# Earlier tile chains in the output projection, and seven products in place of eight for the second gate and up block

## The chip, the cores and the metric

The kernel runs on one core of a Trainium2 chip. The metric is the device time of one execution in microseconds (us). A core has several engines that run side by side, each working through its own list of instructions in order: TensorE (PE in the profile) multiplies matrices, VectorE (DVE) and ScalarE (ACT) work on elements, GpSimd (POOL) does a few small things here, and SyncE's queue (SP) starts the transfers from memory.

## The reference

One layer of a hybrid network, on 128 prompt tokens and 512 sample tokens, in float32, width 1024. Cut to what matters here:

```python
h = _rms(x, norm_mix) * (1 + sc1) + sh1
mix, k, v = _mixer(h, ...)               # attention and a short convolution, then merged @ w_out
x = x + g1 * mix
h2 = _rms(x, norm_ffn) * (1 + sc2) + sh2
gate, up = jnp.split(h2 @ w_gate_up, 2, axis=-1)      # w_gate_up: 1024 x 5632
x = x + g2 * ((jax.nn.silu(gate) * up) @ w_down)      # w_down: 2816 x 1024
```

## The kernel before

All 640 tokens are handled together, as five tiles of 128 in the order prompt, 0, 1, 2, 3 (`TORD`; below they are the first to the fifth tile). Every float32 matrix is split into a high and a low part (`split`: ScalarE rounds the high part, VectorE subtracts to get the low part), and every product is three matmuls (`mm3`: high by high, high by low, low by high).

**The output projection** runs in two halves of 512 columns (`for j in range(2)`). In the second half (j = 1), for each tile n, TensorE does 24 matmuls into `ab`; then comes what is called a tile chain here: ScalarE scales one half (L1070), VectorE adds the other (L1071), multiplies by the gate `g1` (L1073) and adds the residual (L1074); ScalarE sums the squares (L1079), VectorE, GpSimd and VectorE make the norm (L159, L161, L1081) and leave `x2n`. After the matmuls of tile n, TensorE transposes `x2n` of tile n - 1 (`h2_turn`, L960), and ScalarE (L967) or VectorE (L965, four of the last tile's eight pieces) evicts the pieces with the modulation into `h2`. So the fourth tile's transposes come after the fifth tile's matmuls, and the last tile's transposes come inside the gate and up stage.

**Gate and up** treats 22 blocks f of 128 gate and 128 up columns. Per block, the weights are a 2 by 2 matrix of blocks (A11, A12 for gate, A21, A22 for up; the inner dimension halved) and the activations another (B11 and B21 for tokens 0 to 319, B12 and B22 for tokens 320 to 639). A product of one A block and one B block is 12 matmuls of 320 columns. The first `NPLAIN` = 2 blocks go by the eight plain products (`plain`, once for the low tokens `LO`, once for the high ones `HI`). The others go by seven products (Strassen and Winograd's form): `ff_a` A11 by B11, `ff_c` S1 by T1, `ff_d` S2 by T2, `ff_b` A12 by B21, `ff_e` S3 by T3, A22 by T4 and S4 by B22, `ff_end` the last sums. S1 to S4 are sums of weight blocks, made by VectorE for each f (L203) and split (L147, L148); T1 to T4 are sums of activation blocks, made once (`b_sums`: L1033, then split by L1019 and L1020). `b_plain` splits the B blocks themselves (L1017, L1019, L1020). B12, B22 and T1 to T4 are made in two parts: `two[0]`, tokens 320 to 511, once the fourth tile is there, and `two[1]`, tokens 512 to 639, once the fifth is there.

TensorE's order is written out by hand. At the start of gate and up it is, as the program says it:

```python
b_plain("B12 B22", two[0]); b_sums(two[0])
for x in range(NPLAIN):
    plain(x, ("B11", "B21"), LO)
    if x == 0:
        h2_turn(TORD[-1])
        b_plain("B12 B22", two[1])
b_sums(two[1])
for x in range(NPLAIN):
    plain(x, ("B12", "B22"), HI)
```

(two lines joined in one; the third block, f = 2, follows by seven products.) The orders of VectorE and ScalarE are not written by hand: when the program is built, each engine takes, among the instructions whose inputs are expected to be there, the one that stands first in the program. `early(n)` counts an instruction as if it stood n places earlier. A chain of dependent instructions on one engine lets a waiting one of lower rank in between its links. What is built is a fixed list for each engine.

Weights come through SP's queue into three buffers of 512 KB (`wf`) and are split into eight slots (`wh`, `wl`) in a planned order (`order`, `W`, `op_load`); the same eight slots hold the output projection's weights until its last matmuls. The splits of the first block and of A11 of the second are placed in the program ahead of the chains of the later tiles.

Of the kernel before, what the change touches and what calls it, by code (L numbers as in the profile page):

```python
# [28 lines left out]
HALF = TOK // 2  # L29
# [23 lines left out]
GSP = 30  # L53
FEND = 2
AOP = 9
NPLAIN = 2
QEV = '00001'
PPO = ''
RSP = 0
# [9 lines left out]
PT = 2  # L69
PRB = 4  # L70
PHB = 2
XP = 50
AWB = 2
AO = 6
SOON = 150
# [12 lines left out]
def build(ctx, tc, x_prompt, x_sample, c, cache_k, cache_v, c_ctx, norm_mix, norm_ffn, w_ada, b_ada,  # L88
# [27 lines left out]
    def T(tag, shape, dt=F32, bufs=1):  # L116
        seq[0] += 1
        return pools[where.get(tag, "A")][1].tile(list(shape), dt, tag=tag, bufs=bufs, name=f"{tag}_{seq[0]}")
# [15 lines left out]
    def PS2():  # L134
        return PB((P, 2, 512), tag="s")
# [7 lines left out]
    def early(n):  # L143
        return tc.high_priority(n)

    def split(hi, lo, src):
        act.activation(hi, src, AF.Copy)  # L147
        dve.tensor_tensor(lo, src, f32(hi), ALU.subtract)  # L148

    def mm3(out, lh, ll, rh, rl, start, stop, more=False):  # L150
        pe.matmul(out, lh, rh, start=start, stop=False, skip_group_check=more)  # L151
        pe.matmul(out, lh, rl, start=False, stop=False, skip_group_check=more)  # L152
        pe.matmul(out, ll, rh, start=False, stop=stop, skip_group_check=more)  # L153
# [31 lines left out]
    def plan(key, src, ph=0, ring="w", gain=None):  # L185
        place[key] = len(order)
        order.append([key, src, ph, ring, gain, None])
# [3 lines left out]
    def op_load(e):  # L191
# [4 lines left out]
        if name[0] == "S":  # L196
            if name == "S1":
# [3 lines left out]
                             "S3": (s13, a11, a21, ALU.subtract), "S4": (s24, a12, s24, ALU.subtract)}[name]  # L201
            with early(SOP[f >= NPLAIN]):
                (pool if f < SPO else dve).tensor_tensor(src, x, y, op)  # L203
# [3 lines left out]
        ops[0] += 1  # L207
        with early(SOP[f >= NPLAIN]):
            split(w[:, 0], w[:, 1], src)
# [72 lines left out]

    GROUPS = [list(range(a, b)) for a, b in zip(GCUT, GCUT[1:])]
    PLAIN, PRODS = ("A11", "A12", "A21", "A22"), ("A11", "S1", "S2", "A12", "S3", "A22", "S4")

    def plan_raw(f, x, ph=3):
        col = f * P + (DFF if x == "u" else 0)
        plan((x, f), wg[:, :, col:col + P], ph, "f")

    def plan_ops(f, names, ph=3):  # L290
        for x in names:
            plan(("op", f, x), None, ph, "op")

    G2KP = {0: (0,), 1: (1,), 2: (2, 3)}
    for gi, grp in enumerate(GROUPS):
        for f in grp:
            ph = 2 if f < NPLAIN else 3
            plan_raw(f, "g", ph)
            plan_raw(f, "u", ph)
            plan_ops(f, PLAIN if f < NPLAIN else PRODS, ph)  # L300
        for j in range(2):
            for i0 in range(0, len(grp), 2):
                n = len(grp[i0:i0 + 2])
                plan(("d", grp[i0], j), wd[:, grp[i0]:grp[i0] + n, j * 512:(j + 1) * 512], 2)
                if gi == 0 and j == 0:
                    for kp in G2KP[i0 // 2]:
                        plan(("ada", 5, 1, kp), wa[:, 2 * kp:2 * kp + 2, 5 * D + 512:6 * D], 2, "f")
# [614 lines left out]
    for x in SEQ.split():  # L922
        if "." in x:
            n, i = (int(y) for y in x[1:].split("."))
# [44 lines left out]
    def mix_half(src):  # L969
        mh = T("mH", (P, 4, P), F32R, 4)  # L970
        ml = T("mL", (P, 4, P), F32R, 4)
        split(mh, ml, src)
        return mh, ml
# [34 lines left out]
    def quarter(name, part):  # L1008
        h, c0 = int(name[1]) - 1, HALF * (int(name[2]) - 1)
        return h2[h][:, :, c0 + part.start:c0 + part.stop]  # L1010

    def b_put(name, src, part):
        if name not in B:
            b_tile(name)
        w = B[name][4]
        if name in BHD:
            dve.tensor_copy(w[:, 0, :, part], src)  # L1017
        else:
            act.activation(w[:, 0, :, part], src, AF.Copy)  # L1019
        dve.tensor_tensor(w[:, 1, :, part], src, f32(w[:, 0, :, part]), ALU.subtract)  # L1020

    def b_plain(names, part):
        for x in names.split():
            b_put(x, quarter(x, part), part)

    def b_sums(part):
        n = part.stop - part.start
        b11, b12, b21, b22 = (quarter(x, part) for x in ("B11", "B12", "B21", "B22"))
        last = None
        for x in ("T1", "T2", "T3", "T4"):  # L1030
            w = T("tr", (P, 4, 192), F32, 3)[:, :, :n]
            y, z = {"T1": (b12, b11), "T2": (b22, last), "T3": (b22, b12), "T4": (b21, last)}[x]
            dve.tensor_tensor(w, y, z, ALU.subtract)  # L1033
            b_put(x, w, part)
            if x != "T3":
                last = w

    for j in range(2):
        cols = slice(j * 512, (j + 1) * 512)
        for n, t in enumerate(TORD):  # L1040
            cc = 1 if t == CTX else 0
            c0 = t * P + (2 if t == CTX else 0)
            ms = [mix_ctx if t == CTX else mix_half(of[t]), mix_half(yf[:, :, c0:c0 + P])]
            ab = PS2()
            for half in range(2):
                for p in range(4):
                    wh, wl = W(("o", j, 2 * half + p // 2))
                    mm3(ab[:, half], ms[half][0][:, p], ms[half][1][:, p], wh[:, p % 2], wl[:, p % 2],
                        p == 0, p == 3)
                if j == 0 and CRP == f"{n}{'me'[half]}":  # L1050
                    next(ada_gen, None)
                    conv_rms()
            if j == 1 and n:
                h2_turn(TORD[n - 1])
                if n == 2:
                    b_plain("B11 B21", slice(0, 256))
                if n == 3:
                    b_plain("B11 B21", slice(256, HALF))
            if j == 0 and n == 1:
                att_rms(NL - 1)  # L1060
            if j == 0 and G2N <= n < 4 + G2N:
                g2_step(0, n - G2N)
            if j == 1 and n == 0:
                g2_out(0)
            if j == 0:
                x2[t] = T("x2", (P, D), F32, NT)
                sp.dma_start(x2[t], x_dram[t])
            with early(XP):
                m = T("mix", (P, 512), F32, 2)
                act.activation(m, ab[:, 1], AF.Copy, scale=rB[t])  # L1070
                dve.scalar_tensor_tensor(m, ab[:, 0], rA[t], m, ALU.mult, ALU.add)  # L1071
                e = pool if j == 0 and n < PX else dve
                e.tensor_tensor(m, m, g1[cc][:, cols], ALU.mult)  # L1073
                e.tensor_tensor(x2[t][:, cols], m, x2[t][:, cols], ALU.add)  # L1074
            if j == 1:
                with early(XP):
                    x2n[t] = T("x2n", (P, D), F32, 1)
                    ss = T("ss", (P, 1), F32, 6)
                    act.activation(x2n[t], x2[t], AF.Square, accum_out=ss)  # L1079
                    r = rstd_of(ss, 1, 1.0 / D)  # L1080
                    dve.tensor_scalar_mul(x2n[t], x2[t], r)  # L1081
# [49 lines left out]
    def ff_a(f):  # L1131
        b1 = FB()
        prod(b1, f, "A11", "B11")
        cg = T("cg", (P, TOK), F32, 2)
        st[f] = [b1, copy_of("p1", b1), cg, None, None, None, None]

    def ff_b(f):
        b2 = FB()
        prod(b2, f, "A12", "B21")
        b1, p1, cg = st[f][0:3]  # L1140
        dve.tensor_tensor(cg[:, LO], b2[:, :HALF], p1, ALU.add)
        act.activation(cg[:, LO], cg[:, LO], AF.Silu)
# [69 lines left out]
    for gi, grp in enumerate(GROUPS):  # L1212
        for f in grp:
            if f == 0:
                two = slice(0, 192), slice(192, HALF)
                b_plain("B12 B22", two[0])
                b_sums(two[0])
# [3 lines that stand above are left out]
                        h2_turn(TORD[-1])  # L1221
                        b_plain("B12 B22", two[1])
                        phase[0] = 3
                b_sums(two[1])
                for x in range(NPLAIN):
                    plain(x, ("B12", "B22"), HI)
            elif f >= NPLAIN:
                ff_a(f)
                if f - 1 in st and FEND == 1:
                    ff_end(f - 1)  # L1230
                ff_c(f)
                if f - 1 in st:
                    ff_end(f - 1)
                ff_d(f)
                ff_b(f)
                ff_e(f)
                if f == grp[-1] or FEND == 0:
                    ff_end(f)
        down(gi, grp)
        for f in grp:  # L1240
            del gT[f]
# [52 lines left out]
```

## Time and profile before

| | us |
|---|---|
| median of 3 runs | 765.26 (763.04 to 766.77) |
| the profiled execution's own time | 765.82 |
| its span | 764.1 |
| TensorE busy | 739.6 |
| VectorE busy | 560.2 |
| ScalarE busy | 374.4 |

Times in the trace are counted from the span's start. 1.72 us of the execution lie outside the span. A line of the timeline gives the start, the duration, the engine, the line of the kernel, the operation, its result and its operands, and in brackets how long the engine had been idle and what ended that. Matmuls overlap, so the distance between two starts is what one costs, not the printed duration; the same holds, for under 0.1 us, on VectorE and ScalarE. The change concerns the stretch from about 314 us (the fourth tile's chain) to 357.5 us (start of the block f = 2).

### The profile page before, as it was taken

To read this page: it belongs to the slowest core of one execution; us is meant where nothing else is said; L and a number is where in the kernel's file an instruction comes from. 1 tells how busy PE (TensorE), PEld (TensorE's weight loads), DVE (VectorE), ACT (ScalarE), POOL (GpSimd) and SP (SyncE) were. 2 spreads that over 40 slices of the span, in tenths; PEclk is the share of its full clock that TensorE was granted. 3 is DMA by queue.
4 is the path that set the end of the run, shared out by engine and by line. 5 is a ranking of instruction groups with operands and counts; after the bars stand their busy time and mean duration, and the time that the engine had idled before them with its cause. 6 is when DMAs were issued, how large, how long until landed. Compare 5 with 4: busy or idle time off the path is not lost.

```text
span 764.1 us, 11890 instructions
## 1 busy us (share of the span) xinstructions
PE 739.6 (97%) x4580; PEld 665.5 (87%) x4580; DVE 560.2 (73%) x1009; ACT 374.4 (49%) x712; POOL 48.2 (6%) x77
## 2 busy tenths in 40 slices
PE   4998999999999999899999999999999999999997
PEld 3667988989999887699998789998889998899986
DVE  5566987676566798798779678884578866788653
ACT  5355776666665445865552125553125541255410
POOL 3104201011010130000000000000000000000000
PEclk9999999999999999989999999999999999999999
DMA  9984133423424453121235313233113232222312
GB/s 289 301 241 140 42 111 112 152 90 113 151 90 133 157 179 112 53 59 56 84 109 164 99 56 111 65 102 111 55 56 98 69 111 75 64 84 83 111 55 83
DMA packets 102349, 84.52 MB, mean 111 GB/s; under 512 B 4526, under 2 KB 82674, under 8 KB 102292
## 3 DMA queue, kind: packets, MB, share of 16 engines
q1 hardware_dynamic: 100980, 83.39, 35.8%
q8 instruction: 36, 0.59, 0.3%
q10 hardware_dynamic: 1056, 0.26, 0.2%
q14 instruction: 21, 0.17, 0.1%
q0 software_dynamic: 256, 0.11, 0.1%
HBM read 79.68 MB, written 2.75 MB: 108 GB/s over the span
## 4 chain that ended last, share of the span: by engine, by line
PE 85%; DVE 6%; DMA 3%; ACT 2%; SPq 1%; POOL 1%; issue 1%; ACTq 0%; DVEq 0%; POOLq 0%
PE pf L151 19%; PE pf L153 19%; PE pf L152 19%; PE pc L674 3%; PE pc L675 3%; PE pc L676 3%; PE po L831 2%; PE ps L788 2%; PE pt L814 2%; PE pc L376 2%; DMA af<-in_w_ada_dram 2%; PE ps L151 2%; PE ps L152 2%; PE ps L153 2%; POOL rs L161 1%
## 5 line engine op out<-in xcount | busy, mean ns | idle before, releaser
L147 ACT ACTIVATE wh<-wf 128x1024 fp32r<-128x1024 f32 (+1 forms) x76 | 64.1, 844 | 93.6 <-PE pf L153 63.0
L151 PE MATMUL pf<-wh,gT 128*128 128x512 f32 (+1 forms) x225 | 88.2, 392 | 0.0
L152 PE MATMUL pf<-wl,gT 128*128 128x512 f32 (+1 forms) x225 | 87.8, 390 | 0.0
L153 PE MATMUL pf<-wh,gT 128*128 128x512 f32 (+1 forms) x225 | 87.8, 390 | 0.0
L148 DVE TENSOR_TENSOR wl<-wf,wh 128x1024 fp32r<-128x1024 f32 (+1 forms) x42 | 49.2, 1171 | 29.7 <-ACT wh L147 26.8
L674 PE MATMUL pc<-hH,wh 128*128 128x320 f32 x192 | 61.1, 318 | 0.0
L676 PE MATMUL pc<-hH,wl 128*128 128x320 f32 x192 | 59.4, 309 | 0.0
L675 PE MATMUL pc<-hL,wh 128*128 128x320 f32 x192 | 59.4, 309 | 0.0
L152 PEld LDWEIGHTS pf<-wl,gT 128*128 128x128 f32 x225 | 42.3, 188 | 9.8 <-DVE wl L148 0.2
L151 PEld LDWEIGHTS pf<-wh,gT 128*128 128x128 f32 x225 | 42.2, 188 | 9.9 <-ACT wh L147 0.2
L153 PEld LDWEIGHTS pf<-wh,gT 128*128 128x128 f32 x225 | 42.2, 188 | 9.8
L151 PE MATMUL pf<-T,wl 128*128 128x320 f32 x160 | 49.2, 308 | 0.0
L152 PE MATMUL pf<-T,wl 128*128 128x320 f32 x160 | 49.2, 308 | 0.0
L153 PE MATMUL pf<-T,wl 128*128 128x320 f32 x160 | 49.2, 308 | 0.0
L151 PE MATMUL pf<-T,wh 128*128 128x320 f32 x160 | 49.2, 308 | 0.0
L152 PE MATMUL pf<-T,wh 128*128 128x320 f32 x160 | 49.2, 308 | 0.0
L153 PE MATMUL pf<-T,wh 128*128 128x320 f32 x160 | 49.2, 307 | 0.0
L151 PE MATMUL pf<-B,wl 128*128 128x320 f32 x152 | 47.0, 309 | 0.0
L152 PE MATMUL pf<-B,wl 128*128 128x320 f32 x152 | 46.8, 308 | 0.0
L153 PE MATMUL pf<-B,wl 128*128 128x320 f32 x152 | 46.7, 307 | 0.0
L1207 DVE TENSOR_TENSOR dm<-pf,g 128x512 f32<-128x512 f32 (+1 forms) x41 | 27.7, 675 | 22.9 <-PE pf L153 22.9
L147 ACT ACTIVATE wl<-wf 128x512 fp32r<-128x512 f32 x34 | 21.3, 628 | 46.3 <-PE pf L152 36.8
(281 smaller groups left out, 2059.2 us busy)
## 6 DMA issues: line engine op xcount, KB each, us to landing
wf<-in_w_gate_up_dram SPq DMA_DIRECT2D x44, 512.0 KB, 4.1
aw<-in_w_ada_dram SPq DMA_DIRECT2D x24, 512.0 KB, 4.8
wf<-in_w_down_dram SPq DMA_DIRECT2D x20, 512.0 KB, 3.3
wf<-in_w_in_dram SPq DMA_DIRECT2D x18, 512.0 KB, 6.1
af<-in_w_ada_dram SPq DMA_DIRECT2D x32, 256.0 KB, 6.4
x<-in_x_sample_dram SPq DMA_DIRECT2D x8, 512.0 KB, 4.9
wf<-in_w_out_dram SPq DMA_DIRECT2D x8, 512.0 KB, 4.6
wf<-in_w_ada_dram SPq DMA_DIRECT2D x8, 512.0 KB, 3.8
```

The costliest lines, as they stand in the source:

```text
L147: act.activation(hi, src, AF.Copy)
L148: dve.tensor_tensor(lo, src, f32(hi), ALU.subtract)
L151: pe.matmul(out, lh, rh, start=start, stop=False, skip_group_check=more)
L152: pe.matmul(out, lh, rl, start=False, stop=False, skip_group_check=more)
L153: pe.matmul(out, ll, rh, start=False, stop=stop, skip_group_check=more)
L376: pe.matmul(out[CG * g:CG * (g + 1)], cp[:, k], w, start=(k < 4), stop=(k >= KD - 4), skip_group_check=True)
L674: pe.matmul(acc, wh[:, k], hH[k][:, c0:c0 + n], start=(k == 0), stop=False)
L675: pe.matmul(acc, wh[:, k], hL[k][:, c0:c0 + n], start=False, stop=False)
L676: pe.matmul(acc, wl[:, k], hH[k][:, c0:c0 + n], start=False, stop=(k == KD - 1))
L788: pe.matmul(s2[:, g, :320], q, kk[:, v, P + g * 320:P + (g + 1) * 320], start=(i == 0), stop=(i == 1))
L814: pe.transpose(tp[:, i, h], u[3][h][:, kt * P:(kt + 1) * P], ident)
L1207: dve.tensor_tensor(dm, ps[:, :n], g2[cc][:, oc], ALU.mult)
```

## The change

Two things. In the second half of the output projection the tile chains count as standing 400 places earlier (50 before; the first half keeps 50), and the two `b_plain` calls for B11 and B21 stand 300 places earlier (0 before). And the block f = 1 is computed by seven products: its first two (`ff_a`, `ff_b`) take the place of its four plain products on the low tokens, between the last tile's transposes and the plain products of block 0 on the high tokens, and the other five follow those. Its weight blocks are made in an order of their own, and its loads are planned in the same phase as before.

```diff
-NPLAIN = 2
+NPLAIN = 1
-XP = 50
+XP = [50, 400]
+BP = 300
...
+    FIRST = ("A11", "A12", "S1", "S2", "S3", "A22", "S4")
...
-            ph = 2 if f < NPLAIN else 3
+            ph = 2 if f <= NPLAIN else 3
...
-            plan_ops(f, PLAIN if f < NPLAIN else PRODS, ph)
+            plan_ops(f, PLAIN if f < NPLAIN else FIRST if f == NPLAIN else PRODS, ph)
...
-                if n == 2:
-                    b_plain("B11 B21", slice(0, 256))
-                if n == 3:
-                    b_plain("B11 B21", slice(256, HALF))
+                with early(BP):
+                    if n == 2:
+                        b_plain("B11 B21", slice(0, 256))
+                    if n == 3:
+                        b_plain("B11 B21", slice(256, HALF))
...
-            with early(XP):
+            with early(XP[j]):
                 m = T("mix", (P, 512), F32, 2)
...
-                with early(XP):
+                with early(XP[j]):
                     x2n[t] = T("x2n", (P, D), F32, 1)
...
+                ff_a(NPLAIN)
+                ff_b(NPLAIN)
                 b_sums(two[1])
                 for x in range(NPLAIN):
                     plain(x, ("B12", "B22"), HI)
             elif f >= NPLAIN:
-                ff_a(f)
+                if f > NPLAIN:
+                    ff_a(f)
...
-                ff_b(f)
+                if f > NPLAIN:
+                    ff_b(f)
```

Blocks below `NPLAIN` have their splits counted 20 places earlier, the others 0 (`SOP`), so block 1 loses that too.

## The prediction

> **What bounds the kernel now.** I read the page first, then TensorE's waits, then the timeline around the one long wait, then VectorE in stretches. The page:
>
> ```profile
> span 764.1 us, 11890 instructions
> PE 739.6 (97%) x4580; PEld 665.5 (87%) x4580; DVE 560.2 (73%) x1009; ACT 374.4 (49%) x712; POOL 48.2 (6%) x77
> ...
> wf<-in_w_gate_up_dram SPq DMA_DIRECT2D x44, 512.0 KB, 4.1
> ```
>
> TensorE is busy 97% of the span: a change pays if it takes TensorE work or TensorE waits away, and costs if it adds waits. The average says nothing on VectorE, whose 73% is uneven, as will be seen. Two of TensorE's longest waits (total, times, longest):
>
> ```profile
> PE pt L960 <- DVE x2n L1081: 4.3, 2, 3.9
> PE pc L376 <- DMA af<-in_w_ada_dram: 3.7, 3, 1.5
> ```
>
> The first line is in the stretch that changes: the transposes of the fourth tile wait once for 3.9 us. TensorE's timeline there, and a shorter wait early in the run for comparison:
>
> ```profile
> 40.88 0.64 PE L376 MATMUL pc<-af,cp 128*32 128x256 f32 x8 [1.53 <-DMA af<-in_w_ada_dram]
> ...
> 320.96 0.39 PE L153 MATMUL ps<-wh,mL 128*128 128x512 f32 x1
> 325.26 1.94 PE L960 MATMUL pt<-ident,x2n 128*128 128x128 f32 x8 [3.91 <-DVE x2n L1081]
> 326.85 0.61 PE L151 MATMUL pf<-B,wh 128*128 128x320 f32 x1
> ...
> 332.07 0.31 PE L151 MATMUL pf<-B,wh 128*128 128x320 f32 x1
> ...
> 335.59 1.03 PE L960 MATMUL pt<-ident,x2n 128*128 128x128 f32 x8
> 336.38 0.39 PE L151 MATMUL pf<-B,wh 128*128 128x320 f32 x1
> ```
>
> From 332.07 to 335.59 lie the last 24 matmuls of block 0 on the low tokens: 0.1467 us each, so 1.76 us for a product of 12 and 7.04 us for four products. Eight transposes cost 0.79 (335.59 to 336.38). From 325.26 to 335.59 TensorE did 8 transposes and 48 matmuls in 10.33 us; at those rates it is 7.83. So 2.50 us were lost behind the wait. The stretches show why, and how full VectorE (third pair of numbers: DVE) is:
>
> ```profile
> 40.90:44.00 3.10, 3.10 (x19) 2.23 (x20) 2.12 (x4) 1.16 (x3) 0.00 (x0) 1.00 1.06 308
> 314.60:321.30 6.70, 6.70 (x34) 5.28 (x32) 6.67 (x10) 6.41 (x16) 0.00 (x0) 1.00 0.03 8
> 325.20:330.30 5.10, 5.04 (x21) 5.07 (x22) 4.83 (x8) 3.92 (x11) 0.00 (x0) 0.50 0.61 181
> ...
> 321.40:340.50 19.10, 15.24 (x92) 15.27 (x93) 18.08 (x31) 14.68 (x29) 1.21 (x2) 0.82 0.37 108
> 340.50:350.00 9.50, 9.50 (x67) 9.50 (x66) 9.38 (x17) 4.91 (x10) 0.00 (x0) 1.00 0.00 0
> ```
>
> The granted clock was 0.50 for 5.1 us after the wait of 3.91, and 1.00 after the wait of 1.53. And VectorE is full: 6.67 of 6.70, 18.08 of 19.10 and 9.38 of 9.50 us. From 314.6 to 350 it has 1.2 us to spare. Here it is not hidden; it is one step behind TensorE.
>
> **Part one, the chains go first.** The fourth tile's chain now:
>
> ```profile
> 314.89 0.69 ACT L1070 ACTIVATE mix<-ps,rB 128x512 f32<-128x512 f32 x1 [0.69 <-PE ps L153]
> ...
> 315.03 2.35 DVE L1020 TENSOR_TENSOR B<-gT,B 128x1024 fp32r<-128x1024 f32 x2
> 317.30 0.74 DVE L1071 SCALAR_TENSOR_TENSOR mix<-ps,rA,mix 128x512 f32<-128x512 f32 x1
> ...
> 321.09 0.68 DVE L1074 TENSOR_TENSOR x<-mix,x 128x512 f32<-128x512 f32 x1
> ...
> 324.35 0.76 DVE L1081 TENSOR_SCALAR x2n<-x,rs 128x1024 f32<-128x1024 f32 x1 [0.44 <-POOL rs L161]
> 325.02 0.75 DVE L1071 SCALAR_TENSOR_TENSOR mix<-ps,rA,mix 128x512 f32<-128x512 f32 x1
> 325.69 0.69 DVE L148 TENSOR_TENSOR wh<-wf,wh 128x512 fp32r<-128x512 f32 x1
> 326.29 0.69 DVE L1073 TENSOR_TENSOR mix<-mix,g 128x512 f32<-128x512 f32 x1
> ```
>
> L1071 could have begun at about 315.6, but two splits of B blocks stood ahead; L1074 ends at 321.77 instead of about 318, for weight splits. With the priority the first B split runs to 316.2 (half of 2.35), and the three links with one foreign instruction of about 0.6 between them, as the rows 325.02 to 326.29 still show, end by 319.4 (318.2 without). From there to x2n took 324.35 + 0.76 - 321.77 = 3.3 us, some 0.6 of it queueing. That puts x2n between 320.9 and 322.7 and, with the 0.15 from x2n's end at 325.11 to the transposes, the wait of 3.91 becomes nothing to 1.5; the full 3.91 stays if more slips in. I take 1.5, since the rows show that others do slip in. A wait of 1.53 left the clock at 1.00, so the half-rate stretch goes too. B11's and B21's splits and the weights of block 0 are in time as before; they only change places with the chain. Then the last tile's transposes start not at 335.59 but at 321.35 + 1.5 + 0.79 + 7.04 = 330.7. So far 4.9 us are won.
>
> **Part two, seven products.** One product of 12 matmuls goes: 1.76 us of TensorE. VectorE gets work: four sums of weight blocks, three more splits, and six sums on results in place of two. ScalarE gets three splits and three copies, some 3 us, and has 4.4 us free from 321.4 to 340.5 alone. A block's transfers stay two, but S4's sum now reads the gate buffer late, so the third block's up weights load behind it in SP's queue, with the later loads behind them; S4's sum done at about 340 and 4.1 us to land, they are there by 344 and are not needed before 360.
>
> But the order decides. Between the last tile's transposes and the first use of B12 there were four products, 7.04 us; now there are two, 3.52. TensorE wants B12 at 330.7 + 0.79 + 3.52 = 335.0. When is it there? VectorE's rows of now:
>
> ```profile
> 339.10 1.36 DVE L965 TENSOR_SCALAR gT<-pt,modA,modB 128x128 f32<-128x128 f32 x4
> 340.58 0.69 DVE L1020 TENSOR_TENSOR gT<-gT,gT 128x512 fp32r<-128x512 f32 x1
> 341.19 0.42 DVE L1017 CAST B<-gT 128x512 fp32r<-128x512 f32 x1
> 341.53 0.68 DVE L203 TENSOR_TENSOR sx<-wf 128x512 f32<-128x512 f32 x1
> 342.13 0.68 DVE L1020 TENSOR_TENSOR B<-gT,B 128x512 fp32r<-128x512 f32 x1
> ...
> 349.27 0.68 DVE L1020 TENSOR_TENSOR T<-tr,T 128x512 fp32r<-128x512 f32 x1
> ```
>
> The last tile's transposes were done at about 336.5, yet its evictions on VectorE began at 339.10 and B12's low part ended at 341.27, 2.1 us before TensorE came for it at 336.38 + 7.04 = 343.4. VectorE got to them late because T1 to T4 and the weight splits stand ahead in the program. They still do, and the change moves TensorE forward without taking a single VectorE instruction from in front of them. If all 1.02 us of idling went, B12 would be ready at 340.25. It adds, ahead of them, the four sums of block 1 at 0.60 each (341.53 to 342.13): 2.4 us; the two splits of S1 and S2 replace those of A21 and A22 and cost nothing extra. So B12 is ready at 340.25 + 2.4 = 342.65. Bounds: with only S1 and S2 ahead of it, 341.45; with all idling kept and the first result sum of block 1 (0.4) ahead too, 344.1. I take 342.65, since both the sums and the evictions stand in a row on a full engine; B12's low part is asked for by the second matmul, so the product starts at 342.5.
>
> TensorE thus waits about 7.5 us, with everything of the kernel behind it; whatever the chains win ahead of it only makes this wait longer. After 3.91 the clock was halved for 2.50 us of loss, and I charge that again. Four products on the high tokens (7.04) and five of block 1 (8.80) follow: the third block starts at 342.5 + 7.04 + 8.80 + 2.50 = 360.8. Before, it started at 336.38 + 144 x 0.1467 = 357.5. The change costs 3.3 us. T1 to T4's second parts and the splits of S3, A22 and S4 are VectorE work after B12, about 1.4 us later than before (T4's at 349.95 then); TensorE wants T1 at 352.0 and T4 at 357.3, so they are covered, by 2 us or more. After the third block nothing changes.
>
> [...]
>
> Against the profiled execution's own 765.82 (span 764.1) the sum is 769.1; the median of the runs is 0.56 below that execution, so I forecast 768.6.
>
> **The rivals.** *VectorE serves the last tile first* (faster). The order on VectorE comes from expected readiness, and it may come out so that the evictions and B12 precede T1 to T4. Then TensorE goes on at 335.0 and T4 is next: 349.95, less the 1.0 of idling, less five instructions of the third block and of block 1's plain form that stood before it (2.8), plus 2.8 of new sums and two splits (1.2): 350.1; with the two products from A22 by T4 on, 3.52, the third block starts at 353.6, 3.9 earlier: 761.4. The deciding point is B12 ready by 339.2 with the clock halved, 341.7 without. For it: T1 to T4 are made in links, with gaps. Against: in the trace the links were filled with each other. Chance 0.13.
>
> *The clock does not fall.* If the wait breaks into two, say one before A12 by B21, whose split loses 20 places, neither part may be long enough. Then the third block starts at 358.3: 0.8 slower, 766.1. [...] Chance 0.22.
>
> *The weight sums and T parts are late too* (slower still). If the third block's sums and splits get ahead of T3 and T4's second parts and of S3's split, four or five instructions of 0.6 delay TensorE again by some 2.5 us: 771.1. For it: VectorE's 9.38 of 9.50 up to 350. Chance 0.17.
>
> **How the numbers follow.** The forecast has 0.48. Its own range, from the bounds on B12, is 767.4 to 770.1. Half a per cent is 3.83 us, about what a measurement of this kernel can tell from no change; its edges are 761.4 and 769.1. Two fifths of the forecast case and the last rival lie above, with a little from the clock case: slower 0.42. The first rival sits at the lower edge: faster 0.09. Within: 0.49. The range goes from 761.5 to 772, leaving out half of the first rival and the tail of the last.
>
> **What would show it.** Right: the wait for x2n under 2 us and the clock at full rate behind it; a wait of 6 to 8 us in front of A11 by B12, on B12 or on the evictions that feed it, with VectorE full up to that point and the clock near 0.5 after it; the third block starting at about 361. Wrong: B12 ready by 339, or no TensorE wait over 3.5 us, or VectorE idle while TensorE waits.

## The result, and the profile after

| | before | after |
|---|---|---|
| median of 4 runs each, us | 764.45 (763.04 to 766.77) | 772.36 (771.77 to 775.43) |
| ratio | | 1.0105, 95% interval 1.0085 to 1.0124 |
| profiled execution's own time | 765.82 | 772.78 |
| start of the third block (f = 2) | 357.50 | 364.02 |

The kernel became slower by 1%, where 768.6 with a range up to 772.0 was forecast. The page of the changed kernel, then TensorE's waits (total, times, longest):

```profile
span 770.6 us, 11878 instructions
PE 740.4 (96%) x4568; PEld 663.5 (86%) x4568; DVE 565.8 (73%) x1020; ACT 377.0 (49%) x718; POOL 48.5 (6%) x77
```

```profile
PE pf L154 <- DVE wl L149: 4.5, 1, 4.5
PE pf L152 <- ACT gT L1021: 3.9, 1, 3.9
...
PE pt L962 <- ACT gT L969: 0.9, 2, 0.6
...
PE pt L962 <- DVE x2n L1084: 0.5, 2, 0.4
```

Twelve matmuls are gone (4580 to 4568), and VectorE has 11 instructions and 5.6 us more (560.2 to 565.8; 1009 to 1020). The long wait for x2n is gone, but two of 4.5 and 3.9 us are new. TensorE's timeline shows where (L152 to L154 are the three matmuls of `mm3`, L962 the transposes, L999 a landmark used below):

```profile
322.24 0.63 PE L962 MATMUL pt<-ident,x2n 128*128 128x128 f32 x4 [0.32 <-ACT gT L969]
323.49 0.66 PE L962 MATMUL pt<-ident,x2n 128*128 128x128 f32 x4 [0.62 <-ACT gT L969]
...
331.02 1.03 PE L962 MATMUL pt<-ident,x2n 128*128 128x128 f32 x8
...
338.63 0.64 PE L154 MATMUL pf<-B,wl 128*128 128x320 f32 x1 [4.52 <-DVE wl L149]
...
345.52 0.64 PE L152 MATMUL pf<-gT,wh 128*128 128x320 f32 x1 [3.86 <-ACT gT L1021]
...
358.63 0.42 PE L152 MATMUL pf<-T,wh 128*128 128x320 f32 x1 [0.53 <-ACT u L1131]
...
364.02 0.31 PE L152 MATMUL pf<-B,wl 128*128 128x320 f32 x1
...
434.31 1.88 PE L999 MATMUL pt<-cg,ones 128*128 128x512 f32 x4
```

The output projection ends where the fourth tile's transposes begin, less their wait: 322.24 - 0.32 = 321.92 (before: 325.26 - 3.91 = 321.35). The last tile's transposes start at 331.02, and 0.57 of that is the later end of the output projection. Then A12 by B21 waits 4.52 for the low part of A12, and the first product of block 0 on the high tokens waits 3.86 for B12. The windows show the clock (the last figure but two) ahead of both and behind each of them, and VectorE (third pair):

```profile
321.90:334.10 12.20, 11.26 (x79) 10.78 (x78) 11.76 (x20) 10.67 (x22) 0.99 (x1) 1.00 0.29 85
338.60:341.70 3.10, 3.04 (x10) 2.64 (x10) 2.38 (x4) 0.00 (x0) 0.00 (x0) 0.51 0.00 0
345.50:350.50 5.00, 4.89 (x22) 4.54 (x23) 5.00 (x10) 2.20 (x4) 0.00 (x0) 0.66 0.19 57
```

It was halved twice: 0.51 over 3.1 us, and 0.66 over 5.0 us, the first 2.5 of them at 0.50. The balance from the end of the output projection to the third block, at 0.1467 a matmul and 0.79 for eight transposes:

| us | before | forecast | after |
|---|---|---|---|
| TensorE's work | 29.74 | 27.98 | 27.98 |
| waits | 3.91 | 1.5 + 7.5 | 0.94 + 4.52 + 3.86 + 0.53 |
| slow matmuls | 2.50 | 2.50 | 0.33 + 1.81 + 2.13 |
| sum | 36.15 | 39.5 | 42.10 |

The third row is what remains of each piece: 331.02 - 321.92 less work and waits is 0.33, 345.52 - 331.02 leaves 1.81, 364.02 - 345.52 leaves 2.13. The whole loss is in these 42 us: 5.95 here, of 6.5 in the span, with 0.57 ahead of it. By the medians it is 7.9: the profiled executions lie 1.4 (before) and 0.4 (after) above theirs, and 0.46 more of the changed one's time lies outside its span.

VectorE's rows in front of B12, and the one of ScalarE that holds them up:

```profile
335.29 2.69 DVE L1022 TENSOR_TENSOR T<-tr,T 128x768 fp32r<-128x768 f32 x3
337.89 0.68 DVE L149 TENSOR_TENSOR wl<-wf,wl 128x512 fp32r<-128x512 f32 x1
...
340.30 0.68 DVE L204 TENSOR_TENSOR sx<-wf,wf 128x512 f32<-128x512 f32 x1
342.41 0.69 DVE L149 TENSOR_TENSOR wl<-wf,wl 128x512 fp32r<-128x512 f32 x1 [1.43 <-ACT wl L148]
343.02 0.48 DVE L1114 TENSOR_TENSOR cu<-pf,cg 128x320 f32<-128x320 f32 x1
343.42 0.68 DVE L149 TENSOR_TENSOR wh<-sx,wh 128x512 fp32r<-128x512 f32 x1
344.02 1.36 DVE L967 TENSOR_SCALAR gT<-pt,modA,modB 128x128 f32<-128x128 f32 x4
345.50 0.69 DVE L1022 TENSOR_TENSOR gT<-gT,gT 128x512 fp32r<-128x512 f32 x1
```

```profile
341.75 0.63 ACT L148 ACTIVATE wl<-wf 128x512 fp32r<-128x512 f32 x1 [3.79 <-PE pf L154]
```

A12's low part (337.89) is made only behind the first parts of T1 to T4. Then VectorE itself waits 1.43 at 342.41: the next split, A22's, needs a weight slot that A12 by B21 gives back, and that product had waited for VectorE and then ran at half clock (0.51). ScalarE's row shows it, released by TensorE at 341.75. The last tile's evictions, whose transposes were done since 332, stand behind all this in the list and begin at 344.02; B12's low part ends at 346.19.

### The profile page after: what moved, and what is told of

The parts are those of the page before. It is cut to its first block, busy times and chain, and to the rows that moved or that the text cites. A ratio compares the mean times of both kernels' runs of the same rounds, so it can differ in the third digit from the quotient of the medians.

```text
span 770.6 us, 11878 instructions
## 1 busy us (share of the span) xinstructions
PE 740.4 (96%) x4568; PEld 663.5 (86%) x4568; DVE 565.8 (73%) x1020; ACT 377.0 (49%) x718; POOL 48.5 (6%) x77
## 5 line engine op out<-in xcount | busy, mean ns | idle before, releaser
L152 PE MATMUL pf<-wh,gT 128*128 128x512 f32 (+1 forms) x225 | 88.1, 391 | 0.0
L154 PE MATMUL pf<-wh,gT 128*128 128x512 f32 (+1 forms) x225 | 87.6, 389 | 0.0
L152 PE MATMUL pf<-T,wh 128*128 128x320 f32 x168 | 51.8, 308 | 0.5 <-ACT u L1131 0.5
L152 PE MATMUL pf<-T,wl 128*128 128x320 f32 x168 | 51.8, 308 | 0.2 <-ACT p L1131 0.2
L153 PE MATMUL pf<-T,wh 128*128 128x320 f32 x168 | 51.7, 308 | 0.0
L153 PE MATMUL pf<-T,wl 128*128 128x320 f32 x168 | 51.7, 308 | 0.0
L154 PE MATMUL pf<-T,wh 128*128 128x320 f32 x168 | 51.7, 307 | 0.0
L154 PE MATMUL pf<-T,wl 128*128 128x320 f32 x168 | 51.7, 307 | 0.0
L152 PEld LDWEIGHTS pf<-wh,gT 128*128 128x128 f32 x225 | 42.2, 187 | 9.9 <-issue 0.2
L154 PEld LDWEIGHTS pf<-wh,gT 128*128 128x128 f32 x225 | 42.2, 187 | 9.9
L148 ACT ACTIVATE wl<-sx 128x512 fp32r<-128x512 f32 x41 | 25.8, 629 | 48.7 <-PE pf L153 35.4
L154 PE MATMUL pf<-B,wl 128*128 128x320 f32 x140 | 43.9, 313 | 4.5 <-DVE wl L149 4.5
L152 PE MATMUL pf<-B,wl 128*128 128x320 f32 x140 | 43.5, 311 | 0.0
L153 PE MATMUL pf<-B,wl 128*128 128x320 f32 x140 | 43.5, 311 | 0.0
```

## The experiments

What lies ahead of the stretch moves by a few us from profile to profile (the output projection ended between 320.4 and 323.3), so each profile is also read by the **stretch**: from the end of the output projection to the landmark at L999, `cg,ones`. Before it is 427.86 - 321.35 = 106.51, after 434.31 - 321.92 = 112.39. The stretches of the table come from the same two rows of each trace, VectorE's total from its page. "Seven" and "eight" are the products of block 1.

| kernel | block 1 | median | ratio to before, 95% interval | stretch against before | VectorE |
|---|---|---|---|---|---|
| after | seven | 772.36 | 1.0105, 1.0085 to 1.0124 | +5.88 | 565.8 |
| e1_chains_only | eight | 764.1 | 0.9988, 0.9972 to 1.0005 | -0.84 | 559.9 |
| e2_seven_only | seven | 770.44 | 1.0076, 1.0053 to 1.0099 | +4.80 | 565.2 |
| e3_block1_20 | seven | 770.87 | 1.0085, 1.0068 to 1.0101 | +4.82 | 565.5 |
| e4_last_tile_first | seven | 769.77 | 1.0069, 1.0051 to 1.0086 | +4.31 | 564.6 |
| e5_both | seven | 770.28 | 1.0067, 1.0042 to 1.0092 | +4.04 | 565.7 |
| e7_both_pool | seven | 770.32 | 1.0061, 1.0039 to 1.0082 | +4.97 | 564.0 |
| e8_sums_pool | seven | 772.19 | 1.0090, 1.0063 to 1.0117 | +5.87 | 563.6 |
| e9_scalar_relief | seven | 767.44 | 1.0028, 1.0013 to 1.0043 | +1.70 | 563.1 |
| e10_sums_twice | seven | 772.3 | 1.0101, 1.0065 to 1.0138 | +5.94 | 567.9 |
| e11_more_cover | seven | 770.37 | 1.0070, 1.0048 to 1.0093 | +3.83 | 565.0 |
| e6_chains_last | eight | 763.01 | 0.9973, 0.9958 to 0.9988 | -2.49 | 559.9 |
| e12_chains_relief | eight | 762.63 | 0.9970, 0.9956 to 0.9984 | -3.21 | 558.2 |

**Part one alone.** Block 1 goes back to eight products; the chains and the B splits keep their priority.

```diff
-NPLAIN = 1
+NPLAIN = 2
```

> Part one alone: the chains and the B11 and B21 splits stand earlier, both first blocks by eight products. Both theories (the waits come from the order of VectorE's list; or from VectorE simply being full): the wait of 3.91 us for x2n goes and the clock stays at 1.00 behind it (6.4 us); VectorE has B12 at 340.3 to 341.3 and TensorE comes for it at about 338.5, so 2 to 3 us are given back there. 2.3 to 3.5 us faster than before. If the chains do not gain, no change.

Not told apart from before (0.9972 to 1.0005). The wait for x2n and the half clock behind it are gone, as in the changed kernel (1.00 from 325.2 to 330.3 in both), but B12, now wanted at 339.66 - 1.90 = 337.76 and not at 343.4, is late:

```profile
339.66 0.42 PE L152 MATMUL pf<-gT,wh 128*128 128x320 f32 x1 [1.90 <-ACT gT L1020]
340.39 0.61 PE L153 MATMUL pf<-gT,wh 128*128 128x320 f32 x1 [0.31 <-DVE gT L1021]
...
339.60:344.70 5.10, 4.73 (x20) 4.50 (x21) 5.02 (x9) 1.20 (x4) 0.00 (x0) 0.67 0.00 0
```

The first two rows are TensorE's timeline, the third is a window. A wait of 2 to 3 us was foreseen here, a fall of the clock was not, and it fell (0.67 over 5.1 us). Of the 2.3 to 3.5 us expected, 0.84 is left in the stretch; some 2 went into slow matmuls behind this wait (of the 3.91 + 2.50 lost before, less 0.84, there remain 5.57; the waits are 0.94 and 2.21, and 0.33 lies ahead).

**Part two alone.** The priorities are those of before.

```diff
-XP = [50, 400]
-BP = 300
+XP = [50, 50]
+BP = 0
```

> Part two alone: the second block by seven products, the chains at 50 places as before. Both theories: the wait of 3.91 us for x2n is there again, and a wait in front of A12 by B21 or A11 by B12 as well, since it is this part that makes it: 4 to 8 us slower than before. If the loss needed both parts together, within 2 us of before.

Part two alone carries the loss (+4.80 of stretch). Its fourth tile waits 4.69 for x2n again, and so TensorE is later everywhere and waits less behind it:

```profile
325.14 1.94 PE L962 MATMUL pt<-ident,x2n 128*128 128x128 f32 x8 [4.69 <-DVE x2n L1084]
...
339.94 0.42 PE L154 MATMUL pf<-B,wl 128*128 128x320 f32 x1 [1.68 <-DVE wl L149]
...
344.16 0.41 PE L152 MATMUL pf<-gT,wh 128*128 128x320 f32 x1 [2.49 <-ACT gT L1021]
344.89 0.42 PE L153 MATMUL pf<-gT,wh 128*128 128x320 f32 x1 [0.31 <-DVE gT L1022]
...
344.10:348.00 3.90, 3.52 (x22) 3.30 (x23) 3.76 (x7) 1.20 (x4) 0.00 (x0) 1.00 0.52 150
```

(Timeline and, last, a window.) 4.69 + 1.68 + 2.49 + 0.31 are 9.17; the changed kernel's waits up to the same place, 0.94 + 4.52 + 3.86, are 9.32. This is a first hint, no more, that the sum is fixed by something other than TensorE's order.

**Is it the order of VectorE's list?** Theory at this point: two instructions stand too late in it, the split of A12 and the last tile's evictions, and moving them frees TensorE. e3 gives block 1 its 20 places back (at the weight sums, shown here, and at the splits):

```diff
-            with early(SOP[f >= NPLAIN]):
+            with early(SOP[f > NPLAIN]):
```

> The changed kernel, with block 1's weight sums and splits counted 20 places earlier again (as they were by eight products). Order theory: the low part of A12 is split before T1 to T4, the wait of 4.52 us in front of A12 by B21 goes with its half-rate stretch; the evictions stay late, so a wait of 4 to 6 us before A11 by B12 remains: 3 to 4 us faster than the changed kernel, 4 to 5 slower than before. Load theory (VectorE is full, whatever the order): the first wait only moves into the second, within 1 us of the changed kernel.

e4 lets the last tile's evictions and the B12 and B22 parts count 150 places earlier (inside `h2_turn` the second argument goes to an `early` around the evictions):

```diff
-                        h2_turn(TORD[-1])
-                        b_plain("B12 B22", two[1])
+                        h2_turn(TORD[-1], LAST)
+                        with early(LAST):
+                            b_plain("B12 B22", two[1])
```

> The changed kernel, with the last tile's evictions and its part of B12 and B22 counted 150 places earlier. Order theory: the wait of 3.86 us before A11 by B12 goes, the one before A12 by B21 stays or grows to 5 to 7 us, since A12's split now stands behind them too: 1 to 4 us faster than the changed kernel. Load theory: within 1 us of the changed kernel.

And e5 does both.

> The changed kernel, with block 1's sums and splits 20 places earlier and the last tile's evictions and its part of B12 and B22 150 places earlier, both at once. Order theory (each alone only handed the wait on to the other): TensorE now waits 3 to 4 us, once, before A11 by B12, and perhaps 1 us before S1 by T1: 2 to 4 us faster than either alone, 0 to 3 slower than before. Load theory: the sum of TensorE's waits stays at 7.5 to 8.5 us and the time within 1 us of either alone.

TensorE's long waits in this stretch, a fence for each of the three:

```profile
344.67 0.64 PE L152 MATMUL pf<-gT,wh 128*128 128x320 f32 x1 [8.37 <-ACT gT L1021]
```

```profile
340.78 0.64 PE L155 MATMUL pf<-B,wl 128*128 128x320 f32 x1 [7.54 <-DVE wl L150]
```

```profile
339.27 0.63 PE L153 MATMUL pf<-gT,wh 128*128 128x320 f32 x1 [3.88 <-ACT gT L1023]
...
350.46 0.42 PE L153 MATMUL pf<-T,wh 128*128 128x320 f32 x1 [1.31 <-ACT T L1023]
351.40 0.41 PE L154 MATMUL pf<-T,wh 128*128 128x320 f32 x1 [0.53 <-DVE T L1024]
```

The theory falls. In e3 the wait for A12 is gone and 4.52 and 3.86 have become a single 8.37 for B12. In e4 B12 is in time and A12's split is later: 7.54. In e5 both are sooner, and T1, which was never late, is now. Each order serves what it was told to serve and is late with what it passed; the stretch gets 1.1 to 1.8 us shorter, not the 5.9 that was lost.

**Is it VectorE's load?** Second theory: whatever the order, VectorE is full up to where the last of these parts is wanted, and seven products ask it for some 5 us more in there (up to the landmark it is busy 91.64 us before and 96.56 after). Then only work taken off VectorE helps, about one for one, and work put on costs as much. From e5, e9 gives ScalarE four of the last tile's evictions and the B21 and B22 copies; e10 computes S1 and S3 of block 1 three times each.

```diff
-H2E = [0, 0, 0, 2, 0]
-BHD = ("B21", "B22")
+H2E = [0, 0, 0, 0, 0]
+BHD = ()
```

> Both reorderings, and some of VectorE's work given to ScalarE: the last tile's four evictions (1.36 us on VectorE) and the high parts of B21 and B22 (0.69, 0.28, 0.55 and 0.42). Load theory: at least 2.2 us less on VectorE ahead of the places where TensorE waits, so its 6.8 us of waits shrink to 4.5 to 5 and the time by 2 to 3 us. Rival (ScalarE becomes what is late, or the order decides): within 1 us of both reorderings.

```diff
                 dve.tensor_tensor(src, x, y, op)
+                if f == NPLAIN and name in ("S1", "S3"):
+                    dve.tensor_tensor(src, x, y, op)
+                    dve.tensor_tensor(src, x, y, op)
```

> Both reorderings, with the sums S1 and S3 of block 1 each computed three times: four more VectorE instructions of 0.60 us in the stretch, the suspected cost enlarged by 2.4 us. Load theory: 2 to 2.5 us slower than both reorderings. Rival (VectorE has room, only the order matters): within 1 us of them.

The pages' lines, e5 first, then e9, then e10:

```profile
PE 742.7 (97%) x4568; PEld 665.5 (87%) x4568; DVE 565.7 (74%) x1020; ACT 376.8 (49%) x718; POOL 48.4 (6%) x77
```

```profile
PE 737.3 (96%) x4568; PEld 662.1 (87%) x4568; DVE 563.1 (74%) x1012; ACT 380.1 (50%) x726; POOL 49.1 (6%) x77
```

```profile
PE 740.5 (96%) x4568; PEld 664.8 (86%) x4568; DVE 567.9 (74%) x1024; ACT 377.0 (49%) x718; POOL 48.3 (6%) x77
```

VectorE's load went down by 2.6 us and the stretch by 2.34 (4.04 to 1.70; medians 770.28 to 767.44, both against their own runs of before). It went up by 2.2 and the stretch by 1.90 (to 5.94; median 772.3). That is 0.9 us per us in both directions. Counted up to the landmark alone, VectorE is busy 96.23 us in e5, 93.83 in e9 and 98.97 in e10, which makes it 1.0 and 0.7. Each stretch is that of one profile. By the runs e9 and e10 are clearly apart (up to 1.0043 and from 1.0065), but e10's interval overlaps e5's and e9's just touches it: the direction is shown, the size per us is rough.

How the time is lost is another matter. e9:

```profile
322.18 1.07 PE L963 MATMUL pt<-ident,x2n 128*128 128x128 f32 x8 [1.78 <-ACT gT L971]
...
339.71 0.47 PE L153 MATMUL pf<-gT,wh 128*128 128x320 f32 x1 [4.91 <-ACT gT L1023]
340.44 0.64 PE L154 MATMUL pf<-gT,wh 128*128 128x320 f32 x1 [0.26 <-DVE gT L1024]
```

e9's waits up to the third block are 7.48 in all (with a later one of 0.53) and e5's 7.76: nearly the same. From B12's first matmul to the 0.53 wait on `u` lie six products, 10.56 at full rate. After their waits e5 took 3.45 longer than that, e9 1.88: most of the gain came out of slow matmuls. B12 itself came later in e9 (its first matmul 19.31 us after the end of the output projection, 17.55 in e5), so the gain is not that the evictions left B12's own chain. The reading that fits is that waits and slow matmuls trade against each other, since a slow TensorE gives VectorE time, and that only their sum follows VectorE's load; no run varied the clock alone, so this is argued.

VectorE was not wholly full, either. In e5 it idled 1.68 us at 346.85, for a split of ScalarE's, which had waited 2.09 for TensorE, and TensorE's clock was 0.50 from 339.2 to 344.3. In e10 it idled 0.70 at 346.30, and in e9 nowhere more than 0.21 from the last tile's norm to the last T part. Part of what e9 won can be this idling.

**Would more cover on TensorE help?** If the loss came from the two products that seven products take out from in front of B12, two others in their place would win it back. e11 brings A11 by B11 and A12 by B21 of the third block to there (with one more buffer for their results, and their splits and loads sooner).

```diff
-                ff_a(NPLAIN)
-                ff_b(NPLAIN)
+                for x in (NPLAIN, NPLAIN + 1):
+                    ff_a(x)
+                    ff_b(x)
```

> Both reorderings, and A11 by B11 and A12 by B21 of the third block too before the products on the high tokens, their weights loaded and split for that: TensorE has four products between the last tile's transposes and B12 again, 7.04 us in place of 3.52, none of which needs T1 to T4. If the lost cover is what costs (load theory): the wait before A11 by B12 falls from 3.9 to 0 to 2 us and 3 to 4 us are won over both reorderings, about level with the kernel before or 1 us slower. Rival (VectorE's total up to T4 decides, cover or not): the wait moves to S1 by T1 and T3, under 1.5 us won.

```profile
342.49 0.41 PE L153 MATMUL pf<-gT,wh 128*128 128x320 f32 x1 [1.55 <-ACT gT L1033]
...
358.38 0.42 PE L153 MATMUL pf<-T,wh 128*128 128x320 f32 x1 [4.32 <-ACT u L1143]
```

The wait for B12 shrank from 3.88 to 1.55, and 4.32 appeared later, at a product with a T part. What it waited for last is not that part but ScalarE's copy of a result (`u`, at 357.90), which stood in ScalarE's list behind splits that had waited for VectorE (0.51, 0.57 and 0.38). The stretch is 3.83 against e5's 4.04, where 3 to 4 us were hoped for. Cover moved the wait and didn't remove it; since the edit also brought splits of the third block forward on VectorE, it did not vary the cover alone.

**Could GpSimd take the sums?** From e5 (e7) and from the changed kernel (e8), with S1 to S4 of block 1 on GpSimd.

```diff
-SPO = 0
+SPO = 2
```

> Both reorderings, and the weight sums S1 to S4 of block 1 on GpSimd in place of VectorE (four instructions of 0.60 us less on VectorE). Load theory: another 2 to 2.5 us faster than both reorderings alone. Order theory: GpSimd's slower sums (its 512-column rows took 1.6 us here) come in time, and the wait shrinks only by what stood ahead of B12, 1 to 2 us; if they come late, TensorE waits at S1 by T1 instead.

> The changed kernel with only the sums S1 to S4 of block 1 on GpSimd in place of VectorE; the order else as it falls. Load theory: TensorE's waits shrink by 2.4 us in all, 2 to 3 us faster than the changed kernel. Order theory: A12's split and the evictions stand behind the same things, under 1.5 us faster.

No gain: 770.32 and 772.19 against 770.28 and 772.36. VectorE's total fell by 1.7 and 2.2, and by the load theory 2 to 3 us should have been won. The timeline of e7, GpSimd and VectorE, shows what stood against it:

```profile
323.09 3.67 POOL L205 TENSOR_TENSOR sx<-wf 128x512 f32<-128x512 f32 x1 [3.35 <-DMA wf<-in_w_gate_up_dram]
326.83 1.29 POOL L205 TENSOR_TENSOR sx<-sx,wf 128x512 f32<-128x512 f32 x1
328.08 0.56 POOL L163 TENSOR_TENSOR rs<-ms,neghalf 128x1 f32<-128x1 f32 x1
...
328.67 0.75 DVE L1086 TENSOR_SCALAR x2n<-x,rs 128x1024 f32<-128x1024 f32 x1 [2.56 <-POOL rs L163]
...
330.54 1.78 DVE L150 TENSOR_TENSOR wl<-sx,wl 128x512 fp32r<-128x512 f32 x1
...
333.11 1.64 DVE L1021 CAST B<-gT 128x768 fp32r<-128x768 f32 x1
```

A sum that takes 0.68 on VectorE took 1.29 to 3.67, the last tile's norm (328.08) queued behind two of them, VectorE idled 2.56 for it (2.57 in e8), and two of VectorE's own instructions were stretched (1.78 where 0.68 is usual, 1.64 where 0.55). Each of the two began while GpSimd was at a sum and ended 0.4 to 0.5 us after that sum did (at 331.78 and 334.34). Others that ran beside a sum kept their time (0.68 at 324.05, 0.95 at 332.24); the trace shows the stretching, not its cause. So e7 and e8 speak neither for the load theory nor against it.

**Eight products and the last tile first.** What is left is part one with room made for B12: e1 with e4's edit.

> Part one alone, with the last tile's evictions and its part of B12 and B22 150 places earlier. T1 to T4 are not needed before the third block here, so putting B12 ahead of them costs nothing: the wait of 1.90 + 0.31 us and the half clock behind it go, 3 to 4 us faster than part one alone, 4 to 5 us faster than before. If VectorE's load decides here too: a wait of about the same size turns up at the third block's T1, and the time is that of part one alone.

```profile
340.64 0.41 PE L153 MATMUL pf<-gT,wh 128*128 128x320 f32 x1 [0.18 <-ACT gT L1022]
341.62 0.41 PE L154 MATMUL pf<-gT,wh 128*128 128x320 f32 x1 [0.57 <-DVE gT L1023]
```

763.01, faster than both kernels (0.9958 to 0.9988 against before); e1's 1.90 and 0.31 are 0.18 and 0.57 and the clock stays whole (1.00 over the next 5 us). It is 2.3 us below the median of before, where 4 to 5 were expected: a wait of 1.04 for a block's results has turned up at 360.42. With e9's relief on top (four evictions go to ScalarE, not the two that the expectation names):

> The second gate and up block stays at eight products (part one alone), the last tile's evictions and B12, B22 are served first, and in addition VectorE is relieved of two of the last tile's evictions and of two rounding copies in each of three blocks, which go to ScalarE. Load theory: VectorE's list is shorter in the full stretch, so what is left of TensorE's waits there (0.18 + 0.57 for B12 and 1.04 for block 1's results in the kernel without the relief) goes or shrinks, and the time is 0.5 to 1.5 us below that kernel's 763.0, so 761.5 to 762.5, some 3 to 4 us below the kernel before. Rival: the load decides only where TensorE really waits for VectorE, and ScalarE, at 15.25 of 18 us between 322 and 340 already, now releases the transposes' PSUM buffers later (1.78 us there in the relieved kernel with seven products, against 0.94): then it is 763 to 764.5, no better.

```profile
323.68 1.06 PE L962 MATMUL pt<-ident,x2n 128*128 128x128 f32 x8 [1.77 <-ACT gT L970]
...
340.85 0.42 PE L154 MATMUL pf<-gT,wh 128*128 128x320 f32 x1 [0.64 <-DVE gT L1023]
```

762.63, the lowest median, but its interval lies on e6's, so the two are not told apart. By the stretch it wins 0.72: B12 waits 0.64 in place of 0.75 and the wait of 1.04 at 360.42 is gone, while the fourth tile's transposes wait 1.77 for ScalarE's evictions, 0.83 more. Here 1.7 us less on VectorE bring less than half of it, since TensorE no longer waits for VectorE for long.

## Why the prediction was right or wrong

- **Slower, by a wait for B12 that part two makes: right in kind.** The mechanism is in the trace, but the wait did not stand in one place: 7.5 was forecast in front of A11 by B12, and it was 3.86 there and 4.52 in front of A12 by B21. The size was off: the forecast cost of 3.3 us up to the third block was 5.95.
- **The step that failed: "So B12 is ready at 340.25 + 2.4 = 342.65."** It was ready at 346.19, or 345.6 with the 0.57 of the earlier difference taken off: 3.0 late, and beyond the upper bound of 344.1. The term counted the four sums alone. In the trace the splits of A22 (342.41) and S3 (343.42) stand in front as well, 0.6 each, VectorE idles 1.43 for a slot, and 0.44 of idling for the norm (328.93), which the term took as gone, is still there: 3.1 together. e3, where the idling for the slot is gone, had B12's low part at 345.34, or 344.0 on before's times: the bound itself. The error behind it was to count only what I saw placed ahead of B12. The total could have been counted: 11 more instructions (four sums, three splits, four result sums), which came to 5.6 us in the profile. I took those behind B12 to be covered "by 2 us or more"; in e9 and e10 a us of VectorE in this stretch cost 0.7 to 1.0. Neither moved only work that stands behind B12, so that such work costs as much is argued.
- **A12's low part was taken as in time; it cost 4.52.** I saw it under the rival "The clock does not fall" ("A12 by B21, whose split loses 20 places"), as a reason for a shorter loss. It split the wait, but the clock fell at both halves.
- **The half clock, charged once at 2.50, came twice: 1.81 and 2.13.** With waits of 9.85 against 9.0 forecast, the balance is 0.85 more waiting and 1.77 more slow matmuls. The clock fell behind 4.52 and behind 3.86, but in e1 also behind 1.90 with 0.31 (0.67 over 5.1 us); no length of wait that decides it is shown.
- **Part one: right in the trace.** 1.5 was taken as left of the 3.91; it was 0 for x2n, but 0.94 for the transposes' buffers, which ScalarE's evictions of the tile before give back late, and 0.33 more. The last tile's transposes started at 331.02 - 0.57 = 330.45 (forecast 330.7). e1 shows that this gain is taken back by B12 even without part two, as the text said ("only makes this wait longer").
- **The rival "VectorE serves the last tile first", 761.4, was mis-priced.** It did not happen here; built in e4 and e5, it gave 769.77 and 770.28. It let T4 be ready at 350.1 on the count of a few instructions; in e5 the product with T1 itself waited to 350.46.
- **The rival "The weight sums and T parts are late too": wrong for this kernel** (0.53 in front of 358.63, and that for a copied result), right in e5 and e10, where B12 was served first.

## What to carry to other kernels

Where the second engine has no idle time left, price a change by all the work that it adds to that engine in the full stretch, not by what stands ahead of one wait: here 5.6 us more on VectorE cost 5.9 of stretch, although TensorE saved 1.76. Reordering a full list mostly chose which consumer waits (8.37, 7.54, or 3.88 and 1.31 and 0.53) and won back 1.1 to 1.8 of those 5.9; it paid where what it put back was not wanted soon (e6). And a slot that the waiting engine must give back can make the full engine idle too (1.43 us here). Test such a reading by load: add some work, take some away, and see whether the time follows.

## What the runs showed of the hardware that was not expected

The granted clock does not go by the length of the last wait alone. It fell after 1.90 and 0.31 us (0.67 over the next 5.1 us, e1) and stayed at 1.00 after 2.49 and 0.31 (344.1 to 348.0, e2), after 1.55 and 0.31 (342 to 348, e11) and after 1.77 (324 to 330, e12). No kernel here varied one wait alone, so what decided in e1 stays open. Runs of one and the same kernel differ in the clock too: in the session of e9 to e11 the kernel before took 763.01 us at a mean clock of 0.998 and 768.06 at 0.989. So what a fall of the clock costs in a single profile may be in part chance.
